# FFN products of a float32 kernel: one 512-column matmul for both input parts over the high weights, and the down product by output tiles behind all gate and up products

## The chip, the cores and the metric

One core of one Trainium2 chip. The time is device microseconds of one launch on that core, the median of several runs; profiles are of one execution.

## The reference

Two transformer blocks in float32 on 256 tokens of width 1024, with a hidden width of 2816 in the feed-forward networks (FFN). What the change touches are five FFNs:

```python
def conv_ffn(h, w_up, dw_w, dw_b, w_down):          # block 1, once
    u = causal_dwconv(h @ w_up, dw_w) + dw_b        # 3 taps over tokens
    gt, v = jnp.split(u, 2, axis=-1)
    return (jax.nn.silu(gt) * v) @ w_down

def swiglu(x, w_gate, w_up, w_down):                # block 2, four times
    return (jax.nn.silu(x @ w_gate) * (x @ w_up)) @ w_down
...
x = layer_norm(ALPHA * x + 0.5 * swiglu(x, ...), g, b)
```

Around them stand a conformer convolution module (first block), an RWKV-7 mixer with memory attention and a stick-breaking attention with memory attention (second block), and a norm over features after each part.

## The kernel before

Activations lie feature-major: 128 features on partitions, 8 tiles (`KD`) of 256 tokens (`T`). TensorE works on fp32r operands, and each float32 operand is split in a high part, rounded to fp32r, and a low part, the rest. A product of two such operands is three matmuls, high x high, high x low and low x high; low x low is left out. That is `mm3` (L359 to L363): weights stationary (128x128), the activation moving (256 columns).

Weights come as units of 128x1024 float32 in the order of use, two to a DMA of 1 MB on SP's queue (`Stream`, L191). ScalarE casts a unit to its high part `whi` (L229), VectorE subtracts to get the low part `wlo` (L238). `take()` hands out the next unit and issues the splits of the units up to four ahead (`LEAD`); there are 7 buffers for `whi`, 6 for `wlo`. A unit feeds 24 matmuls in every product.

An FFN (`ffn`, L631) goes over 22 hidden tiles j. For each: two units, gate and up, through `gemm_out` into the two halves of one PSUM bank `gu` (48 matmuls), then one unit of the down product of tile j-2 through `gemm_acc` into all 8 output tiles, which are held in 4 banks `acc` (24 matmuls), then the gate of tile j. `ffn_gate` (L672) makes silu(gate) x up on ScalarE and VectorE in three steps and splits it into `hh` and `hl`; its steps are issued between the products (`advance`), so that the engines' queues don't block. The first two tiles run together in `gemm_outs` (L378), one input tile after the other, as the norm before delivers them. The last four hidden tiles are added in `gemm_tail` (L420), one output bank after the other, so that the first output tiles go through their residual add and their squares while the others are still in product.

`Norm` (L1109) sums outputs and squares over tiles: tiles 0 to 3 on GpSimd, 4 and 6 on VectorE, `merge` adds the two, tiles 5 and 7 go as they are; `finish` (L1150) sums over partitions with matmuls of one column on TensorE, issues 12 products that nothing uses (L348), computes the deviation, and broadcasts it over partitions with transposes into `bc` (L1188). `ln_out` (L522) and, in the conv FFN, `rms_scale` apply it tile by tile (L530, L555), and the next product starts on the first tile.

In PSUM there are 8 banks: 2 `gu`, 4 `acc`, 2 for statistics. The order of all work is written out by hand; each engine runs its queue in order.

Of the kernel before, what the change touches and what calls it, by code (L numbers as in the profile page):

```python
# [76 lines left out]
def constants():  # L77
    """Masks and selectors, which depend on the shapes only."""
# [23 lines left out]
def lay_out(inp, parts=ALL):  # L102
    """Host layout: every array sent holds input elements only, reordered."""
# [25 lines left out]
    def ffn(g, u, w):  # L129
        g, u, dn = out_major(g), out_major(u), k_major(w)  # L130
        o = []
        for j in range(NF):
            o += [g[j], u[j]]
            if 0 <= j - 2 < NF - 4:
                o.append(dn[j - 2])
        return np.concatenate([np.stack(o), tail(w)])
# [54 lines left out]
class Stream:  # L191
    """Weight units in the order of use: loaded ahead two by two, then split into two fp32r parts."""
# [18 lines left out]
    def split(self, upto):  # L211
        """split units below upto; ScalarE is one unit ahead of VectorE."""
# [33 lines left out]
    def take(self, ahead=True):  # L246
        """(hi, lo) of the next unit."""
# [6 lines left out]
class Builder:  # L254
# [26 lines left out]
    def open_x(self):  # L281
        """the operand tiles of the dense products; closed where a mixer needs their space."""
        self.xpool = ExitStack()
        xp = self.xpool.enter_context(self.pool("x", side="right"))
        self.xh, self.xl = (xp.tile([P, KD, T], F32R, name=n) for n in ("xh", "xl"))

# [17 lines left out]
    def enter_dense(self, tmp=True):  # L304
        """PSUM banks for the accumulators and the statistics."""
# [28 lines left out]
    def fill(self, n, warm):  # L334
        """n steps of the memory's products, while TensorE would wait for a norm."""
# [5 lines left out]
    def keep_warm(self, n):  # L341
        """products that nothing uses: the clock of TensorE halves when it idles."""
# [8 lines left out]
    def pump(self, us):  # L351
        """issue background work of VectorE for about this long."""
# [6 lines left out]
    def mm3(self, out, wh, wl, xh, xl, start, stop):  # L359
        mm = self.nc.tensor.matmul  # L360
        mm(out, lhsT=wh, rhs=xh, start=start, stop=False, skip_group_check=True)  # L361
        mm(out, lhsT=wh, rhs=xl, start=False, stop=False, skip_group_check=True)  # L362
        mm(out, lhsT=wl, rhs=xh, start=False, stop=stop, skip_group_check=True)  # L363

    def gemm_out(self, ps, xh, xl):
        """one output tile of 128 features from the next unit."""
        for _ in self.gemm_out_parts(ps, xh, xl):
            pass

    def gemm_out_parts(self, ps, xh, xl):  # L370
        wh, wl = self.stream.take()
        for k in range(KD):
            c = slice(k * P, k * P + P)
            self.mm3(ps, wh[:, c], wl[:, c], xh[:, k, :], xl[:, k, :], k == 0, k == KD - 1)
# [3 lines left out]
    def gemm_outs(self, banks, xh, xl):  # L378
        """two output tiles in each bank, from the input tiles as they come."""
        mm = self.nc.tensor.matmul  # L380
        ws = [self.stream.take() for _ in range(2 * len(banks))]
        for k in range(KD):
            c = slice(k * P, k * P + P)
            for q in range(3):
                for i, (wh, wl) in enumerate(ws):
                    mm(banks[i // 2][:, i % 2, :], lhsT=(wh, wl, wh)[q][:, c],  # L386
                       rhs=(xh, xh, xl)[q][:, k, :], start=k == 0 and q == 0 and i % 2 == 0,
                       stop=k == KD - 1 and q == 2, skip_group_check=True)

    def gemm_tok(self, ps, xh, xl, u):  # L390
# [1620 lines left out]
```

## Time and profile before

| | us |
|---|---|
| runs | 1525.16, 1525.85, 1528.46; median 1525.85 |
| profiled execution, from the first to the last instruction | 1528.2 |
| TensorE busy in it | 1472.2 |
| VectorE, ScalarE, GpSimd busy in it | 987.6, 788.0, 86.5 |

Of the profiled execution only the span from the first to the last instruction is given, so it is set against the median of the runs by its ratio. Engines work side by side, so busy times don't add up. TensorE has two rows: PE for matmuls, PEld for weight loads, which run under matmuls. Matmuls are pipelined, and their durations overlap: the time that one costs is the distance from its start to the next one's.

### The profile page before, as it was taken

The page shows a single profiled execution, that of the slowest core. Times are in us where ns is not written, and L with a number is a line of the kernel's source. Part 1 is how long each engine was busy: PE and PEld are TensorE (multiplying, and loading weights), DVE is VectorE, ACT ScalarE, POOL GpSimd, SP SyncE. Part 2 cuts the span into 40 slices and gives each one's busy share as a digit, 9 for nine tenths or more (in the row PEclk, how much of TensorE's full clock was granted, in tenths as well). Part 3 has the DMA queues.
Part 4 walks back from the last instruction along what each step waited for, and adds up shares of the span by engine and source line. Part 5 has one row for each costly group of instructions (what it writes and reads, how often), then busy time and mean ns, then how long its engine had stood idle before and what let it go on. Part 6 is the DMA issues. An engine that isn't in the chain of part 4 may idle for free.

```text
span 1528.2 us, 30494 instructions
## 1 busy us (share of the span) xinstructions
PE 1472.2 (96%) x13109; PEld 1416.0 (93%) x13109; DVE 987.6 (65%) x1493; ACT 788.0 (52%) x1251; POOL 86.5 (6%) x74
## 2 busy tenths in 40 slices
PE   8888899999999999989999999999999999999997
PEld 7867899999999998878889999999999988999997
DVE  8897787776655458985567555575454855664554
ACT  7697466665544446530245444454444566454443
POOL 1110100000000010130010000100000111100001
PEclk9999899999999999999989999999999999999998
DMA  9785366563655543320034555445554433265540
GB/s 384 267 269 200 112 228 228 178 208 112 218 174 188 193 138 132 111 84 3 2 111 169 190 190 176 160 165 184 180 190 166 147 111 104 90 232 184 192 166 28
DMA packets 39161, 250.66 MB, mean 164 GB/s; under 512 B 4337, under 2 KB 4849, under 8 KB 12274
## 3 DMA queue, kind: packets, MB, share of 16 engines
q1 hardware_dynamic: 38594, 247.60, 46.6%
q8 instruction: 102, 1.67, 0.4%
q10 hardware_dynamic: 432, 1.11, 0.2%
q14 instruction: 33, 0.27, 0.1%
HBM read 247.65 MB, written 1.05 MB: 163 GB/s over the span
## 4 chain that ended last, share of the span: by engine, by line
PE 81%; DVE 12%; ACT 4%; issue 2%; POOL 1%; DMA 0%; DVEq 0%; ACTq 0%; POOLq 0%
PE gu L361 14%; PE gu L363 13%; PE gu L362 13%; PE acc L361 7%; PE acc L362 7%; PE acc L363 7%; PE acc L386 3%; DVE wlo L238 2%; PE r L1653 2%; PE st L1161 1%; DVE mraw L570 1%; PE gu L1236 1%; PE gu L348 1%; DVE ys L530 1%; ACT whi L229 1%
## 5 line engine op out<-in xcount | busy, mean ns | idle before, releaser
L238 DVE TENSOR_TENSOR wlo<-wraw,whi 128x1024 fp32r<-128x1024 f32 x416 | 512.4, 1239 | 294.2 <-PE gu L363 152.1
L229 ACT CAST whi<-wraw 128x1024 fp32r<-128x1024 f32 x416 | 430.0, 1047 | 186.7 <-PE gu L362 116.8
L361 PE MATMUL gu<-xh,whi 128*128 128x256 f32 x1824 | 516.1, 283 | 0.0
L363 PE MATMUL gu<-xh,wlo 128*128 128x256 f32 x1824 | 511.5, 280 | 0.0
L362 PE MATMUL gu<-xl,whi 128*128 128x256 f32 x1824 | 508.0, 278 | 0.0
L361 PEld LDWEIGHTS gu<-xh,whi 128*128 128x128 f32 x1824 | 343.2, 188 | 8.8 <-issue 8.4
L362 PEld LDWEIGHTS gu<-xl,whi 128*128 128x128 f32 x1824 | 343.3, 188 | 0.7 <-issue 0.7
L363 PEld LDWEIGHTS gu<-xh,wlo 128*128 128x128 f32 x1824 | 342.4, 188 | 0.0
L362 PE MATMUL acc<-hl,whi 128*128 128x256 f32 x880 | 248.8, 283 | 0.1
L361 PE MATMUL acc<-hh,whi 128*128 128x256 f32 x880 | 248.9, 283 | 0.0
L363 PE MATMUL acc<-hh,wlo 128*128 128x256 f32 x880 | 248.5, 282 | 0.0
L362 PEld LDWEIGHTS acc<-hl,whi 128*128 128x128 f32 x880 | 168.0, 191 | 0.4 <-DVE hl L700 0.3
L363 PEld LDWEIGHTS acc<-hh,wlo 128*128 128x128 f32 x880 | 168.1, 191 | 0.0
L361 PEld LDWEIGHTS acc<-hh,whi 128*128 128x128 f32 x880 | 167.7, 191 | 0.1
L695 ACT ACTIVATE sg<-gu 128x256 f32<-128x256 f32 x80 | 30.7, 384 | 159.6 <-PE gu L363 159.6
L1138 POOL TENSOR_TENSOR nsum<-ys 128x512 f32<-128x512 f32 (+1 forms) x9 | 12.2, 1359 | 1178.9 <-ACT ys L1121 1178.9
L698 ACT CAST hh<-h 128x256 fp32r<-128x256 f32 x110 | 44.7, 407 | 62.5 <-DVE h L697 62.5
L570 DVE TENSOR_TENSOR mraw<-mraw,cact 128x1024 f32<-128x1024 f32 x48 | 60.0, 1252 | 0.4 <-DMA mraw<-in_mod 0.3
L687 DVE SCALAR_TENSOR_TENSOR u<-gu,vecs,u 128x255 f32<-128x255 f32 (+1 forms) x80 | 33.1, 476 | 35.0 <-ACT u L682 35.0
L574 ACT ACTIVATE mraw<-mraw 128x1024 f32<-128x1024 f32 x48 | 50.4, 1054 | 4.2 <-DVE mraw L570 4.2
L700 DVE TENSOR_TENSOR hl<-h,hh 128x256 fp32r<-128x256 f32 x110 | 46.1, 419 | 7.1 <-ACT hh L698 7.1
L697 DVE TENSOR_TENSOR h<-gu,sg 128x256 f32<-128x256 f32 x80 | 33.4, 418 | 20.7 <-ACT sg L695 20.7
(349 smaller groups left out, 2028.5 us busy)
## 6 DMA issues: line engine op xcount, KB each, us to landing
wraw<-in_w SPq DMA_DIRECT2D x208, 1024.0 KB, 4.9
mraw<-in_mod SPq DMA_DIRECT2D x48, 512.0 KB, 5.6
xr<-in_x SPq DMA_DIRECT2D x2, 512.0 KB, 4.1
m<-in_mem SPq DMA_DIRECT2D x1, 1024.0 KB, 8.2
out<-xr SPq DMA_DIRECT2D x3, 256.0 KB, 2.5
cst<-in_consts SPq DMA_DIRECT2D x1, 546.0 KB
lora<-in_lora ACTq DMA_DIRECT2D x1, 384.0 KB, 3.1
lora_g<-in_lora ACTq DMA_DIRECT2D x1, 384.0 KB, 3.8
```

What stands on the lines that cost most here:

```text
L229: b.nc.scalar.copy(out=hi, in_=raw)
L238: b.nc.vector.tensor_tensor(out=lo, in0=raw, in1=hi.bitcast(F32), op=ALU.subtract)
L361: mm(out, lhsT=wh, rhs=xh, start=start, stop=False, skip_group_check=True)
L362: mm(out, lhsT=wh, rhs=xl, start=False, stop=False, skip_group_check=True)
L363: mm(out, lhsT=wl, rhs=xh, start=False, stop=stop, skip_group_check=True)
L386: mm(banks[i // 2][:, i % 2, :], lhsT=(wh, wl, wh)[q][:, c], rhs=(xh, xh, xl)[q][:, k, :], start=k == 0 and q == 0 and i % 2 == 0, stop=k ...
L570: self.nc.vector.tensor_tensor(out=raw, in0=raw, in1=self.cact, op=ALU.mult)
L574: self.nc.scalar.activation(out=raw, in_=raw, func=AF.Copy, accum_out=self.mod[:, j:j + 1])
L687: nc.vector.scalar_tensor_tensor(out=u[i][:, sh:], in0=gu[:, i, :T - sh], scalar=self.vec("f_dw_w", tap * 2 * NF + j + i * NF), in1=u[i][: ...
L697: nc.vector.tensor_tensor(out=h, in0=up, in1=sg, op=ALU.mult)
L698: nc.scalar.copy(out=hh, in_=h)
L700: nc.vector.tensor_tensor(out=hl, in0=h, in1=hh.bitcast(F32), op=ALU.subtract)
```

## The change

The two parts of an activation now lie side by side in one tile, `xx[:, k]` of shape [128, 2, 256], and so do those of a hidden tile, `hx`. Two new helpers: `mm_lo` multiplies the low weights with the high part into the first half of a bank; `mm_wide` does that and then one matmul of 512 columns, high weights with both parts, into the whole bank. So a bank now holds one output tile, in two halves that must be added.

- Gate and up of the four SwiGLU FFNs run through `gemm_wide` (first two tiles `gemm_wides`), each with its own bank; three pairs of banks take turns (`acc` 0 and 1, `acc` 2 and 3, the two `gu`). `wide_gate` copies the second half of each bank with ScalarE and adds the first half with VectorE.
- In the conv FFN gate and up keep three matmuls and one bank.
- In all five FFNs the down product no longer runs between the gates: it follows when all 22 hidden tiles are issued, output tile by output tile, 22 `mm_wide` each, through the four `acc` banks in turn. The steps of the last gate are issued behind products 4 and 8 of the first output tile. The down weights are laid out for this order; a unit still has 8 blocks of 128x128.
- Each output tile adds its two halves as it ends (`on_tile`: in the SwiGLU FFNs two VectorE operations, in the conv FFN a ScalarE copy and a VectorE add), its square follows, and GpSimd sums tiles 0 to 5; tiles 6 and 7 go to the statistics as they are. `gemm_tail` remains for the mixers' output projections.
- The modulation work that was pumped in during the conv FFN's gates (`pump`) is issued between its output tiles.

```diff
+        self.xx = xp.tile([P, KD, 2, T], F32R, name="xx")
+        self.xh, self.xl = self.xx[:, :, 0, :], self.xx[:, :, 1, :]
...
+    def mm_lo(self, out, wl, x, start):
+        self.nc.tensor.matmul(out, lhsT=wl, rhs=x[:, 0, :], start=start, stop=False,
+                              skip_group_check=True)
...
+    def mm_wide(self, bank, wh, wl, x, start, stop):
+        self.mm_lo(bank[:, 0, :], wl, x, start)
+        self.nc.tensor.matmul(bank, lhsT=wh, rhs=x, start=False, stop=stop, skip_group_check=True)
...
+    def gemm_wide(self, bank, x):
+        wh, wl = self.stream.take()
+        for k in range(KD):
+            c = slice(k * P, k * P + P)
+            self.mm_wide(bank, wh[:, c], wl[:, c], x[:, k], k == 0, k == KD - 1)
...
+    def gemm_wides(self, banks, x):
+        ws = [self.stream.take() for _ in banks]
+        for k in range(KD):
+            c = slice(k * P, k * P + P)
+            for bank, (_, wl) in zip(banks, ws):
+                self.mm_lo(bank[:, 0, :], wl[:, c], x[:, k], k == 0)
+            for bank, (wh, _) in zip(banks, ws):
+                self.nc.tensor.matmul(bank, lhsT=wh[:, c], rhs=x[:, k], start=False, stop=k == KD - 1,
+                                      skip_group_check=True)
...
             for j in range(2, NF):
-                gu = self.gu_tile()
+                bk = banks(j)
                 for o in range(2):
-                    self.gemm_out(gu[:, o, :], self.xh, self.xl)
+                    if conv:
+                        self.gemm_out(bk[0][:, o, :], self.xx)
+                    else:
+                        self.gemm_wide(bk[o], self.xx)
                     advance()
-                if acc is None:
-                    acc = [self.acc_tile(i) for i in range(4)]
-                if j - 2 < NF - self.NT:
-                    self.gemm_acc(acc, *hs.pop(0), j == 2)
-                gate(j, gu)
-                if j % 2:
-                    self.pump(1.0)
-            advance()
-            advance()
+                gate(j, bk)
             self.preload(AF.Sqrt)
-            self.gemm_tail(acc, [h[0] for h in hs], [h[1] for h in hs], st, on_tiles)
+            i = 0
+            for o in range(KD):
+                acc = self.acc_tile(o % 4)
+                for j in range(NF):
+                    if i % 8 == 0:
+                        wh, wl = self.stream.take()
+                    c = slice(i % 8 * P, i % 8 * P + P)
+                    self.mm_wide(acc, wh[:, c], wl[:, c], hs[j], j == 0, j == NF - 1)
+                    i += 1
+                    if o == 0 and j in (4, 8):
+                        advance()
+                on_tile(o, acc)
+                st.square(o, o + 1)
+                st.sum(o, o + 1, "pool")
+                if o < KD - 1:
+                    self.pump(3.0)
...
+    def wide_gate(self, banks, j, hh, hl):
+        nc = self.nc
+        lows = self.fp.tile([P, 2, T], F32, name="lows", tag="lows", bufs=2)
+        gs = self.fp.tile([P, 2, T], F32, name="gs", tag="gs", bufs=2)
+        g, u = gs[:, 0, :], gs[:, 1, :]
+        nc.scalar.copy(out=lows[:, 0, :], in_=banks[0][:, 1, :])
+        nc.vector.tensor_tensor(out=g, in0=banks[0][:, 0, :], in1=lows[:, 0, :], op=ALU.add)
+        nc.scalar.copy(out=lows[:, 1, :], in_=banks[1][:, 1, :])
+        nc.scalar.activation(out=g, in_=g, func=AF.Silu)
+        yield
+        nc.vector.tensor_tensor(out=u, in0=banks[1][:, 0, :], in1=lows[:, 1, :], op=ALU.add)
+        nc.vector.tensor_tensor(out=u, in0=u, in1=g, op=ALU.mult)
+        nc.scalar.copy(out=hh, in_=u)
+        yield
+        nc.vector.tensor_tensor(out=hl, in0=u, in1=hh.bitcast(F32), op=ALU.subtract)
...
+        def on_tile(k, ps):
+            y = self.ys[:, k, 0, :]
+            self.nc.vector.scalar_tensor_tensor(out=y, in0=self.xr[:, k, :], scalar=2 * ALPHA,
+                                                in1=ps[:, 1, :], op0=ALU.mult, op1=ALU.add)
+            self.nc.vector.tensor_tensor(out=y, in0=ps[:, 0, :], in1=y, op=ALU.add)
```

## Rows read from the trace of the kernel before

**Rows 1.** The page: busy time of the engines, and the chain that ended last.
```profile
PE 1472.2 (96%) x13109; PEld 1416.0 (93%) x13109; DVE 987.6 (65%) x1493; ACT 788.0 (52%) x1251; POOL 86.5 (6%) x74
PE 81%; DVE 12%; ACT 4%; issue 2%; POOL 1%; DMA 0%; DVEq 0%; ACTq 0%; POOLq 0%
```

**Rows 2.** Busy time by stretch: the conv FFN, then the first SwiGLU FFN.
```profile
core 0: us, PE busy (x) PEld busy (x) DVE busy (x) ACT busy (x) POOL busy (x), PEclk, DMA share, GB/s
181.00:367.00 186.00, 185.11 (x1573) 184.47 (x1571) 144.22 (x223) 116.88 (x182) 2.86 (x3) 1.00 0.56 190
374.00:563.00 189.00, 187.99 (x1584) 187.55 (x1583) 104.83 (x130) 89.37 (x121) 4.37 (x3) 1.00 0.52 179
```

**Rows 3.** Groups by line and shape: count | busy us, mean ns of one.
```profile
L362 PE MATMUL gu<-xl,whi 128*128 128x256 f32 x1824 | 508.0, 278 | 0.0
...
L361 PE MATMUL acc<-hh,whi 128*128 128x256 f32 x880 | 248.9, 283 | 0.0
...
L238 DVE TENSOR_TENSOR wlo<-wraw,whi 128x1024 fp32r<-128x1024 f32 x416 | 512.4, 1239 | 294.2 <-PE gu L363 152.1 <-PE acc L363 49.1 <-issue 45.8
...
L229 ACT CAST whi<-wraw 128x1024 fp32r<-128x1024 f32 x416 | 430.0, 1047 | 186.7 <-PE gu L362 116.8 <-PE acc L362 58.0 <-DMA wraw<-in_w 5.5
...
L697 DVE TENSOR_TENSOR h<-gu,sg 128x256 f32<-128x256 f32 x80 | 33.4, 418 | 20.7 <-ACT sg L695 20.7
L695 ACT ACTIVATE sg<-gu 128x256 f32<-128x256 f32 x80 | 30.7, 384 | 159.6 <-PE gu L363 159.6
```

**Rows 4.** Timeline of TensorE in the first SwiGLU FFN: start us, us.
```profile
429.82 0.28 PE L363 MATMUL gu<-xh,wlo 128*128 128x256 f32 x1
...
434.88 0.28 PE L361 MATMUL acc<-hh,whi 128*128 128x256 f32 x1
...
437.76 0.28 PE L361 MATMUL gu<-xh,whi 128*128 128x256 f32 x1
```

**Rows 5.** Timeline of TensorE in the stick-breaking mixer: float32 products of two passes.
```profile
1224.82 0.59 PE L1966 MATMUL z<-e,sbc 128*128 128x256 f32 x2
1225.25 0.38 PE L1967 MATMUL z<-e,negones 128*128 128x128 f32 x2
1225.47 0.39 PE L1969 MATMUL z<-e,sbc 128*128 128x128 f32 x2
```

**Rows 6.** Groups by line and shape: a float32 pass of 128 columns.
```profile
L1967 PE MATMUL z<-e,negones 128*128 128x128 f32 x24 | 4.6, 274 | 0.0
```

**Rows 7.** The chain that ended last, after the second SwiGLU FFN's down product.
```profile
990.61 1.69 DVE nsum L1138
...
993.14 3.17 PE st L1161 x16
996.31 2.77 PE gu L348 x12
999.08 0.87 PE bc L1188 x4
```

**Rows 8.** Timeline of TensorE there: the last matmul, then one-column matmuls.
```profile
991.31 0.28 PE L363 MATMUL acc<-hh,wlo 128*128 128x256 f32 x1
991.43 0.95 PE L1161 MATMUL st<-inv,ys 128*128 128x1 f32 x8
```

**Rows 9.** Timeline and chain: end of the conv FFN, then of the last FFN.
```profile
366.59 0.28 PE L363 MATMUL acc<-hh,wlo 128*128 128x256 f32 x1
...
371.65 0.44 PE bc L1188 x2
...
1513.40 0.28 PE L363 MATMUL acc<-hh,wlo 128*128 128x256 f32 x1
...
1513.68 2.85 PE st L1161 x24
...
1517.68 1.13 PE bc L1188 x4
```

More of the change, by code (lines that the diff above doesn't have):

```diff
@@ L624, in memory_steps, with ffn, gate @@
         for o in range(2):
-            yield from self.gemm_out_parts(self.mem_ps[0][:, o, :], self.mh, self.ml)
+            yield from self.gemm_out_parts(self.mem_ps[0][:, o, :], self.mx)
             yield
         for u in range(2):
-            yield from self.gemm_tok(self.mem_ps[1], self.mh, self.ml, u)
-    def ffn(self, conv, st, on_tiles):
+            yield from self.gemm_tok(self.mem_ps[1], self.mx, u)
+    def ffn(self, conv, st, on_tile):
         self.mark("ffn")
         with self.pool("ffn") as self.fp:
-            first = [self.acc_tile(2), self.acc_tile(3)]
-            self.gemm_outs(first, self.xh, self.xl)
-            hs, gates = [], []
-            acc = None
-            def gate(j, gu):
-                hs.append([self.fp.tile([P, T], F32R, name=n, tag=n, bufs=self.NT + 1)
-                           for n in ("hh", "hl")])
-                gates.append(self.ffn_gate(gu, j, conv, *hs[-1]))
+            hs = [self.fp.tile([P, 2, T], F32R, name=f"hx{j}") for j in range(NF)]
+            gates = []
+            def gate(j, banks):
+                make = self.conv_gate if conv else self.wide_gate
+                gates.append(make(banks, j, hs[j][:, 0, :], hs[j][:, 1, :]))
                 next(gates[-1])
@@ L649, in advance, with banks @@
                         gates.remove(g)
-            for j, gu in enumerate(first):
-                gate(j, gu)
+            def banks(j):
+                if conv:
+                    return [self.acc_tile(2 + j) if j < 2 else self.gu_tile()]
+                return [self.gu_tile() for _ in range(2)] if j % 3 == 2 else [
+                    self.acc_tile(2 * (j % 3) + o) for o in range(2)]
+            first = [banks(0), banks(1)]
+            (self.gemm_outs if conv else self.gemm_wides)(first[0] + first[1], self.xx)
+            for j, bk in enumerate(first):
+                gate(j, bk)
                 advance()
@@ new lines, in ffn @@
+                gate(j, bk)
+            self.mark("down")
+            self.preload(AF.Sqrt)
+            i = 0
[14 more added lines that the diff above has]
+                    self.pump(3.0)
@@ new lines, in conv_gate @@
+    def conv_gate(self, banks, j, hh, hl):
+        nc = self.nc
+        gu, = banks
+        sg, h = u = [self.fp.tile([P, T], F32, name=f"u{i}", tag=f"u{i}", bufs=2) for i in range(2)]
+        for i in range(2):
+            f = j + i * NF
+            nc.scalar.activation(out=u[i], in_=gu[:, i, :], func=AF.Identity,
+                                 scale=self.vec("f_dw_w", 2 * 2 * NF + f), bias=self.vec("f_dw_b", f))
+        for tap, sh in ((1, 1), (0, 2)):
+            for i in range(2):
+                nc.vector.scalar_tensor_tensor(
+                    out=u[i][:, sh:], in0=gu[:, i, :T - sh],
+                    scalar=self.vec("f_dw_w", tap * 2 * NF + j + i * NF), in1=u[i][:, sh:],
+                    op0=ALU.mult, op1=ALU.add)
+        yield
+        nc.scalar.activation(out=sg, in_=u[0], func=AF.Silu)
+        nc.vector.tensor_tensor(out=h, in0=u[1], in1=sg, op=ALU.mult)
```

127 lines of the change are left out of this document (50 added, 77 removed).

## The prediction

> **What bounds the kernel now.** Read the page first. TensorE is busy for 1472 of 1528 us and holds 81% of the chain that ended last [rows 1]. Second, the table by stretch, for the feed-forward (FFN) stages: in the conv FFN TensorE is busy 185.1 of 186 us, in the first SwiGLU FFN 188.0 of 189 us, at a granted clock of 1.00, which is 2.4 GHz; VectorE there is busy 144 and 105 us, ScalarE 117 and 89 us [rows 2]. So in an FFN nothing but the products counts, and anything else is worth something only where TensorE waits. Five FFNs of about 188 us are 62% of the span.
>
> Third, the groups of instructions, for counts and kinds: 1824 calls of `mm3` from gate, up and input projections, 880 from the down products, each with three matmuls of 256 columns and three weight loads [rows 3]. Fourth, the timeline of TensorE inside an FFN, for the spacing of matmuls, since the durations of 0.28 us overlap: 43 matmuls of gate and up from 429.82 to 434.88 us are 117.7 ns apart, 24 of the down product from 434.88 to 437.76 us are 120.0 ns apart [rows 4]. 256 columns at 2.4 GHz are 106.7 ns. So each matmul costs 11.0 (gate, up) or 13.3 ns (down) above its columns. That excess is what the change works on; the columns stay.
>
> **Part 1: one wide product in place of two.** Before, a step is 3 matmuls x 256 columns; after, it is one of 256 (low weights) and one of 512 (high weights, both input parts). Columns: 768 in both. It is done for gate and up of the four SwiGLU FFNs, 4 x 44 units x 8 = 1408 steps, and for all five down products, 5 x 22 x 8 = 880 steps. The conv FFN's gate and up keep three matmuls, as do the projections.
>
> The trace has no 512-column matmul of this type, so its spacing is bounded. Lower bound: a float32 product of the mixer shows two passes for each call, and its passes take 110 ns for 128 columns (L1967, 0.22 us for two) but 215 ns for 256 (L1966, 0.43 us from 1224.82 to 1225.25) [rows 5], half the column rate. So such a pass over 256 columns lasts as long as 512 columns would here: 512 cycles at 2.4 GHz (213.3 ns) and 2 ns. Upper bound: two of today's, 235.4 (gate, up) or 240 ns (down) [rows 4], no gain. Middle: the excess is paid once per matmul whatever its width: 213.3 + 11.0 = 224.3, or 213.3 + 13.3 = 226.6 ns.
>
> Which of the three is nearest depends on what the excess is. One candidate is the weight load: a matmul of a single column has nothing to stream, and eight of them still take 0.95 us, 0.11 us apart [rows 8], so a weight load alone paces at about 0.11 us; under a 512-column stream it would be hidden, which gives the lower bound. Against it speaks the duration of one matmul: a half-rate pass of 128 columns, also 256 cycles and also with a weight load behind each, lasts 274 ns [rows 6] and starts 110 ns after the one before (0.22 us for two [rows 5]), while the 256-column products last 278 to 283 ns [rows 3]. The stream itself is longer by 4 to 9 ns, not just its wait for weights. I take the middle: fixed for each matmul.
>
> Then gate and up save 11.0 ns x 1408 = 15.5 us and the down products 13.3 ns x 880 = 11.7 us: 27.2 us. At the lower bound a wide matmul replaces 235.4 by 215 and 240 by 215: 20.4 x 1408 + 25 x 880 = 50.7 us. At the upper bound 0.
>
> The Trainium skill (TensorE: Matmul & The Clock Gate, section "Back-to-back issue gap") gives an isolated gap of N/2.4 + 2.5 ns, 262 cycles for 256 columns and 518 for 512. For 256 columns this trace disagrees, 117.7 ns [rows 4] against its 109; for 512 cycles it agrees with the 215 ns of [rows 5]. By that rule the sum would be the 50 us of the lower bound; it is the first rival below.
>
> **Part 2: gates.** A wide bank holds two halves that must be added: `wide_gate` adds two ScalarE copies and two VectorE adds for each j to the two and two there. At 384 and 418 ns [rows 3] that is 22 x 0.8 = 18 us per FFN on each engine. All gate and up work now stands in 22 x 16 steps, 120 us at 342 ns. In it ScalarE does 44 casts (1047 ns), 46 us, plus 22 x 4 x 0.4 = 35 us: 81 of 120 us. VectorE does 44 subtractions (1239 ns), 55 us, plus 37 us: 92 of 120 us. TensorE's own 120 us hides both; three sets of banks in turn give each gate two further j, 11 us, before its bank is wanted. Without that cover the added 18 us would stand in each FFN. In the conv FFN, gate and up alone are 22 x 48 x 117.7 = 124 us; VectorE had 144 us in the whole stage, and 22 of its 66 subtractions (27 us) and the modulation work move to the down part, so less than 117 of 124 us stay. Priced at nothing. The weights come in units of 24 matmuls' worth in either order, and the SP queue loads the same bytes at the same rate: nothing.
>
> **Part 3: the seam.** The first output tile needs all 22 hidden tiles. The last gate's remaining steps are issued behind products 4 and 8 of that tile; its chain (copy, add, Silu, table load, one cast, add, product, cast, subtraction, at 0.4 to 1.3 us) is some 5.5 us, and TensorE comes to product 21 after 21 x 0.345 = 7.2 us. Priced at nothing; if it is 2 us late, 10 us over five FFNs.
>
> **Part 4: the end of each FFN.** Today tiles 4 to 7 end within a few us of each other and VectorE must sum them: after the last matmul of the second SwiGLU FFN (FFN 2) starts (991.31 [rows 8]) the chain shows a VectorE sum of 1.69 us and more, 16 statistics matmuls, 12 fillers of which the last end at 999.08, then the broadcast until 999.95 [rows 7]: 8.64 us. After the change tile 7 ends 7 us behind tile 6, GpSimd has the six sums long before, and what is left is two VectorE steps instead of one, a square (0.42 each), four matmuls (0.7 with their drain), the 1.15 us seen between statistics and broadcast in the last FFN (1516.53 to 1517.68 [rows 9]) and the broadcast, 0.5 to 0.9, with 0.39 for the wide matmul itself and 0.2 of hand-overs: 4.5 us, or 6 if the clock falls and the fillers take 2.8 us as in [rows 7]. FFN 2 saves 2.6 to 4.1 us; the last FFN took 5.41 and the conv FFN 5.50 [rows 9], which leaves 0 to 1 each (in the conv FFN a table load now stands behind the Silu of the last gate); the first and third SwiGLU FFN I put between these, at 1 to 2. Sum 8 us, bounds 4 to 11.
>
> **Sum.** 1528.2 - 27.2 - 8 = 1493.0 us for the profiled execution. Its span is 1528.2 us and the page shows nothing around it; the runs' median is 1525.85, 0.15% below. 1493.0 x 0.9985 = 1491 us.
>
> **Rivals.**
> 1. The excess is the hand-over behind a weight load and vanishes under a long stream (for it [rows 5, 8], against it [rows 3, 6]): 50.7 + 8, so 1528.2 - 58.7 = 1469.5, 1467 us.
> 2. The change does not do what it says: the excess belongs to the columns, a stream at full rate being fed a little too slowly. For it: half-rate streams show almost none [rows 5, 6]. Against it: gate and down differ (117.7 and 120.0) with the same columns. Only part 4 is left: 1518 us.
> 3. Slower: a feed that is too slow may run dry in a long stream. If the wide matmul's second half were read at the half rate of L1966, it would take 107 + 215 = 322 ns, 85 ns above two of today's, and 2288 of them cost 195 us: 1710 us. It decides from 240 ns per wide matmul on, where 3.5 ns x 2288 eats the 8 us of part 4. No row shows such a feed; every 256-column stream lasts about the same.
> 4. The seam and the gates cost what I put at nothing: 10 to 25 us, 1501 to 1516 us.
>
> **How the numbers follow.** Forecast 1491 with chance 0.48 (with 1480 to 1500 as its own range); rival 1 0.28; rival 2 0.11; rival 4 0.08; rival 3 0.05. The range reaches down past rival 1 (bound of part 4: 1464) and up to 1510, which leaves out rivals 2 and 3 and the end of 4. A difference of 0.2% is about what measurement of this kernel can tell from none. Faster 0.91, same 0.04 (rival 2 with nothing from part 4), slower 0.05.
>
> **What would show it.** A wide matmul followed by the next at 224 to 227 ns, and steps of 342 to 347 ns; FFNs of about 181 us against 188; TensorE still busy throughout each FFN, VectorE and ScalarE below it; no wait of TensorE for the last hidden tile; after the last product of an FFN, 4.5 to 6 us to the broadcast. A spacing of 215 would mean rival 1, of 235 rival 2, beyond 240 rival 3; gaps of TensorE on gate tiles rival 4. Wrong above all would be the assumption that the excess is paid per matmul.

## The result, and the profile after

The changed kernel takes 1508.45 us (median of 4 runs, 1506.64 to 1513.66) against 1525.85: 0.9889 of the time before, 95% interval [0.9866, 0.9911]. A second series of it, in the first experiment, gave 1509.08 and 0.9887 [0.9871, 0.9902]. So it is faster by 17 us, 1.1%. The forecast was 1491 us; the direction and the range (1464 to 1510) held, but the gain is just under half of the 35 us worked out.

The page first (the profiled execution spans 1511.9 us):

```profile
PE 1455.1 (96%) x10821; PEld 1300.6 (86%) x10821; DVE 1076.0 (71%) x1701; ACT 832.4 (55%) x1447; POOL 103.3 (7%) x84
...
PE 82%; DVE 12%; ACT 4%; issue 2%; DMA 1%; POOL 0%; DVEq 0%; ACTq 0%; POOLq 0%
```

TensorE is as much the bound as it was in [rows 1]: 2288 matmuls fewer, and only 17 us less of its time. The groups by line and shape (count | busy us, mean ns of one) show what the new matmul is:

```profile
L370 PE MATMUL acc<-hx,whi 128*128 128x512 f32 x880 | 310.8, 398 | 0.0
...
L370 PE MATMUL acc<-xx,whi 128*128 128x512 f32 x832 | 289.6, 390 | 0.0
L358 PE MATMUL gu<-xx,wlo 128*128 128x256 f32 x992 | 278.8, 281 | 0.0
L358 PE MATMUL acc<-hx,wlo 128*128 128x256 f32 x880 | 247.4, 281 | 0.0
```

Durations overlap, so the cost is read from the spacing, as in [rows 4]. The timeline of TensorE in the first SwiGLU FFN, three steps of a gate or up product and three of the down product:

```profile
439.73 0.28 PE L358 MATMUL gu<-xx,wlo 128*128 128x256 f32 x1
439.85 0.39 PE L370 MATMUL gu<-xx,whi 128*128 128x512 f32 x1
...
440.77 0.28 PE L358 MATMUL gu<-xx,wlo 128*128 128x256 f32 x1
...
530.07 0.28 PE L358 MATMUL acc<-hx,wlo 128*128 128x256 f32 x1
530.19 0.40 PE L370 MATMUL acc<-hx,whi 128*128 128x512 f32 x1
...
531.13 0.28 PE L358 MATMUL acc<-hx,wlo 128*128 128x256 f32 x1
```

Three steps take 1.04 us in gate and up and 1.06 in the down product. From the unrounded starts a step (one low and one wide matmul, called a pair below) is 346.7 ns (118.3 low + 228.3 wide) and 353.3 ns (116.7 + 236.7 in the mean). Three matmuls of before took 353.1 and 360.0 ns. So a step saves 6.4 to 6.7 ns, where 11.0 and 13.3 were forecast.

The table by stretch: the conv FFN, ten microseconds inside it, and the first SwiGLU FFN, beside [rows 2]:

```profile
core 0: us, PE busy (x) PEld busy (x) DVE busy (x) ACT busy (x) POOL busy (x), PEclk, DMA share, GB/s
178.00:371.00 193.00, 189.89 (x1428) 181.69 (x1426) 148.92 (x231) 123.29 (x195) 5.43 (x5) 0.99 0.52 189
200.00:210.00 10.00, 7.71 (x53) 7.53 (x53) 8.37 (x15) 7.37 (x13) 0.00 (x0) 0.83 0.36 117
376.50:563.20 186.70, 185.74 (x1060) 162.63 (x1060) 129.30 (x185) 98.85 (x167) 8.22 (x5) 1.00 0.52 186
```

The SwiGLU FFN is full of products, with VectorE and ScalarE well below. The conv FFN has lost TensorE time near 204 us, and some clock with it (0.83 over those ten microseconds). From first to last product (in the conv FFN from the products of the memory on, right behind the broadcast), and from the last matmul's start to the end of the broadcast, in us, each in the one profiled execution:

| FFN | products before | after | end before | end after |
|---|---|---|---|---|
| conv | 189.72 | 192.24 | 5.48 | 4.77 |
| SwiGLU 1 | 189.32 | 186.19 | 7.04 | 4.94 |
| SwiGLU 2 | 188.70 | 185.67 | 8.62 | 4.94 |
| SwiGLU 3 | 188.70 | 185.66 | 6.48 | 5.66 |
| SwiGLU 4 | 188.69 | 185.66 | 5.40 | 4.79 |

SwiGLU products give 12.2 us, the ends 7.9, and the conv FFN takes 2.5 back: 17.6. (The conv FFN also starts 1.1 us later in this execution; the profiled span is 16.3 us shorter.) The end of the second SwiGLU FFN in the timeline, to be held against [rows 7, 8]:

```profile
986.16 0.40 PE L370 MATMUL acc<-hx,whi 128*128 128x512 f32 x1
...
986.40 0.95 PE L1219 MATMUL st<-inv,ys 128*128 128x1 f32 x8
986.60 0.42 DVE L1100 SCALAR_TENSOR_TENSOR ys<-xr,acc 128x256 f32<-128x256 f32 x1 [4.25 <-PE acc L370]
...
987.51 0.42 ACT L1179 ACTIVATE ys<-ys 128x256 f32<-128x256 f32 x1 [5.47 <-DVE ys L1102]
...
988.10 1.03 PE L1219 MATMUL st<-inv,ys 128*128 128x1 f32 x8
...
989.00 1.66 PE L346 MATMUL gu<-whi 128*128 128x256 f32 x12
...
990.50 0.60 PE L1246 MATMUL bc<-head,rn 128*128 128x128 f32 x4
```

VectorE's sum of 1.69 us is gone: it had been idle for 4.25 us when the last tile came. Two adds and a square (L1100, its neighbour L1102, and L1179) run while TensorE does the statistics that were ready before; the last tile's follow at 988.10. 990.50 + 0.60 - 986.16 = 4.94 us against 8.62.

The loss in the conv FFN, in the timeline of all engines:

```profile
201.53 2.00 ACT L226 CAST whi<-wraw 128x1024 fp32r<-128x1024 f32 x2
...
201.99 2.35 DVE L235 TENSOR_TENSOR wlo<-wraw,whi 128x1024 fp32r<-128x1024 f32 x2
...
203.43 1.01 ACT L738 ACTIVATE u<-gu,vecs 128x256 f32<-128x256 f32 x2
...
203.70 0.28 PE L358 MATMUL gu<-xx,wlo 128*128 128x256 f32 x1
...
204.47 1.65 DVE L742 SCALAR_TENSOR_TENSOR u<-gu,vecs,u 128x255 f32<-128x255 f32 x4
...
206.27 0.55 PE L363 MATMUL gu<-xx,whi 128*128 128x256 f32 x1 [2.29 <-ACT u L747]
```

The third gate's steps (L738, L742) stand behind casts and subtractions of weights, 2.00 us on ScalarE and 2.35 on VectorE. They read one of only two banks that gate and up have from there on; TensorE wants that bank again at 203.82; its last reader, L742, ends at 206.12 (the row names L747 as releaser, ScalarE's next step, which ends about then but doesn't read the bank). From the matmul at 203.70 to the next are 2.57 us, 2.45 of them waiting. The granted clock falls to half at the end of that wait (0.50 from 206.2 to 209.6 us, which is 1.2 GHz), and the 14 matmuls behind the one at 206.27 stand 213 ns apart instead of 118.

### The profile page after: what moved, and what is told of

Its sections match the earlier page's. It is cut to its first block, busy times and chain, and to the rows that moved or that the text cites. A ratio compares the mean times of both kernels' runs of the same rounds, so it can differ in the third digit from the quotient of the medians.

```text
span 1511.9 us, 26295 instructions
## 1 busy us (share of the span) xinstructions
PE 1455.1 (96%) x10821; PEld 1300.6 (86%) x10821; DVE 1076.0 (71%) x1701; ACT 832.4 (55%) x1447; POOL 103.3 (7%) x84
## 4 chain that ended last, share of the span: by engine, by line
PE 82%; DVE 12%; ACT 4%; issue 2%; DMA 1%; POOL 0%; DVEq 0%; ACTq 0%; POOLq 0%
PE acc L370 26%; PE acc L358 15%; PE gu L358 7%; PE gu L370 7%; PE gu L363 4%; PE gu L364 3%; DVE wlo L235 2%; PE r L1711 2%; PE acc L412 2%; DVE mraw L595 2%; PE st L1219 1%; PE gu L1294 1%; DVE ys L555 1%; PE gu L346 1%; ACT whi L226 1%
## 5 line engine op out<-in xcount | busy, mean ns | idle before, releaser
L370 PE MATMUL acc<-hx,whi 128*128 128x512 f32 x880 | 310.8, 398 | 0.0
L358 PE MATMUL acc<-xx,wlo 128*128 128x256 f32 x1088 | 292.8, 284 | 2.9 <-ACT xx L561 1.6
L370 PE MATMUL acc<-xx,whi 128*128 128x512 f32 x832 | 289.6, 390 | 0.0
L358 PE MATMUL gu<-xx,wlo 128*128 128x256 f32 x992 | 278.8, 281 | 0.0
L358 PE MATMUL acc<-hx,wlo 128*128 128x256 f32 x880 | 247.4, 281 | 0.0
L358 PEld LDWEIGHTS acc<-xx,wlo 128*128 128x128 f32 x1088 | 201.2, 190 | 8.5 <-ACT xx L561 4.4
L358 PEld LDWEIGHTS gu<-xx,wlo 128*128 128x128 f32 x992 | 187.6, 189 | 0.2
L358 PEld LDWEIGHTS acc<-hx,wlo 128*128 128x128 f32 x880 | 166.1, 189 | 0.0
L363 PE MATMUL gu<-xx,whi 128*128 128x256 f32 x544 | 158.3, 291 | 2.3 <-ACT u L747 2.3
L364 PE MATMUL gu<-xx,whi 128*128 128x256 f32 x544 | 152.6, 281 | 0.0
L1179 ACT ACTIVATE ys<-ys 128x256 f32<-128x256 f32 (+1 forms) x66 | 28.6, 437 | 157.5 <-DVE ys L1102 140.6
L363 PEld LDWEIGHTS gu<-xx,whi 128*128 128x128 f32 x544 | 103.0, 189 | 11.2 <-issue 8.4
L364 PEld LDWEIGHTS gu<-xx,whi 128*128 128x128 f32 x544 | 103.1, 189 | 0.7 <-issue 0.7
L370 PEld LDWEIGHTS gu<-xx,whi 128*128 128x128 f32 x448 | 84.1, 188 | 17.7
L1100 DVE SCALAR_TENSOR_TENSOR ys<-xr,acc 128x256 f32<-128x256 f32 x32 | 13.5, 421 | 95.0 <-PE acc L370 95.0
```

What stands on the lines that cost most here:

```text
L358: self.nc.tensor.matmul(out, lhsT=wl, rhs=x[:, 0, :], start=start, stop=False, skip_group_check=True)
L363: mm(out, lhsT=wh, rhs=x[:, 0, :], start=start, stop=False, skip_group_check=True)
L364: mm(out, lhsT=wh, rhs=x[:, 1, :], start=False, stop=False, skip_group_check=True)
L370: self.nc.tensor.matmul(bank, lhsT=wh, rhs=x, start=False, stop=stop, skip_group_check=True)
L1179: b.nc.scalar.activation(out=b.ys[:, k0:k1, 1, :], in_=y, func=AF.Square)
```

## The experiments

The theories at the start: **A**, the excess over the columns belongs to the columns (rival 2 of the prediction), so a wide matmul has twice of it; **B**, it is paid once for each matmul, as predicted, and what more is seen comes from the other engines' traffic in these stages; **C**, it comes from the place of the operands. Beside them, what the conv FFN's wait and the ends of the FFNs are worth.

**1. The changed kernel, unaltered.**

> The changed kernel once more, unaltered, timed beside the next two. Both theories: 1506 to 1510 us, ratio to the kernel before 0.987 to 0.991.

1509.08 us (1508.1 to 1510.74), ratio 0.9887 [0.9871, 0.9902]. The pause in the conv FFN (193.05 us) is there again, 2.56 us from the start at 202.9 to the next, the step spacings too; the five ends are 4.12, 4.94, 5.79, 4.94 and 4.79 us, 24.6 in all. The pause and the spacings are the kernel's, not one execution's; the ends differ by 0.9 us in single FFNs.

**2. Trains of matmuls on idle tiles,** 96 of each kind, placed behind the last output.

```diff
+            for i in range(N):
+                mm(o[0][:, :256], lhsT=w[:, c(i)], rhs=x[:, i % 8, 0, :], start=i == 0, stop=i == N - 1, skip_group_check=True)
...
+            for i in range(N):
+                mm(o[0], lhsT=w[:, c(i)], rhs=x[:, i % 8], start=i == 0, stop=i == N - 1, skip_group_check=True)
```

> The changed kernel with ten trains of matmuls on idle tiles behind its last output, nothing else running: fp32r of 256, 384 and 512 columns, 512 columns from a second tile, 256 and 512 in turn from either tile, 512 with the same weights throughout, bf16 of 256 and 512. Theory A (the excess over the columns grows with their number, because a stream of 4-byte columns is fed a little slower than 2.4 GHz): 256 at 117 to 120 ns, 384 at about 172, 512 at about 228, whatever the weights, and bf16 512 at about 216. Theory B (the excess is paid once per matmul, and the 228 to 237 ns seen in the changed kernel come from other engines' traffic): 384 at 171, 512 at 224 or below when alone. Theory C (the place of the moving tile counts): the two tiles differ by several ns at the same width.

The timeline of TensorE puts each train in one row, so that the start of the next less its own start, over 96, is the spacing (the window read ends within the train of 384 columns, so that its row counts 11 here):

```profile
1517.82 11.47 PE L1144 MATMUL bo<-xx,bw 128*128 128x256 f32 x96
1529.13 2.11 PE L1146 MATMUL bo<-xx,bw 128*128 128x384 f32 x11
...
1546.09 22.56 PE L1148 MATMUL bo<-xx,bw 128*128 128x512 f32 x96
1568.49 21.95 PE L1150 MATMUL bo<-bh,bw 128*128 128x512 f32 x96
1590.27 0.28 PE L1152 MATMUL bo<-xx,bw 128*128 128x256 f32 x1
...
1679.88 10.65 PE L1160 MATMUL bo<-bhb,bwb 128*128 128x256 bf16 x96
1690.37 20.88 PE L1162 MATMUL bo<-bhb,bwb 128*128 128x512 bf16 x96
```

256 columns: 117.8 ns; 384: 176.7; 512: 233.3 and, from a second tile, 226.9. The same block of weights throughout takes 233.4 for 512 columns, no less than eight blocks in turn. The excess is 11.1, 16.7, and 20.0 or 13.6 ns: it grows with the columns, with every other engine idle. bf16 with the same sizes takes 109.3 and 215.8 (the last from the starts within the train), an excess of 2.5 ns at both widths. For bf16 that is the Trainium skill's isolated gap of N/2.4 + 2.5 (TensorE: Matmul & The Clock Gate, section "Back-to-back issue gap"), 109.2 and 215.8; for the fp32r products of this kernel the runs disagree with it, by 8.6 ns at 256 columns and 11 to 18 at 512. Pairs of a low and a wide matmul took 118.3 + 228.3 from one tile and 116.7 + 236.7 from the other, the kernel's two spacings; which looked like C, and is taken up in 7 to 9. A holds in the main (its 172 for 384 columns was too low); B is out, as 384 and 512 columns exceed its 171 and 224 with nothing else running.

**3. The new order with narrow products:** each wide matmul as two of 256 columns.

```diff
-        self.nc.tensor.matmul(bank, lhsT=wh, rhs=x, start=False, stop=stop, skip_group_check=True)
+        for h in range(2):
+            self.nc.tensor.matmul(bank[:, h, :], lhsT=wh, rhs=x[:, h, :], start=False, stop=stop,
+                                  skip_group_check=True)
```

> Every wide matmul of the changed kernel split again into two of 256 columns with the same weights; order, banks, gates and norm stay as changed. It sets apart what the width gives from what the new order gives. Theory A and B alike by the spacings of the two profiles: steps of 353 ns instead of 346.7 in gate and up, 360 instead of 353 in down, so 1408 x 6.3 + 880 x 6.6 = 14.7 us slower than the changed kernel, about 1523 us, 2 to 4 us under the kernel before. Rival (the new order itself slows the products, by reading the hidden tiles from another place): 1530 us or more.

1523.9 us (1517.74 to 1528.79, 12 runs), ratio 0.9981 [0.9967, 0.9994], against 0.9887 for the changed kernel timed beside it: the width is worth 0.94%, 14.4 us, give or take 3 (each ratio is good to 0.0015). By the spacings of the kernel before it is 1408 x 6.4 ns = 9.0 us for gate and up, 704 x 6.7 = 4.7 for the SwiGLU down products and, by this run's profile, 176 x 4.9 = 0.9 for the conv FFN's (356.0 to 351.1 ns a step): 14.6. This profile shows one thing more: the same three narrow matmuls of gate and up take 353.3 ns in the first and third SwiGLU FFN and 350.0 in the second and fourth, so that its own spacings give 12.6. The new order by itself gains 2.5 us in the medians. In the profiles it gains 7.0: the ends come to 25.2 us (before 33.0), the SwiGLU products are 1.0 us shorter in all, and the conv FFN, which has the pause too (2.66 us at 203.6), is 1.9 longer. But the profile before is of a long execution: 1528.2 us, where the 17 executions of that kernel timed here span 1522.5 to 1529.1. How much of the 7.0 us an average execution has is not shown.

**4. Four banks for gate and up of the conv FFN.** Hidden tiles with j % 4 over 1 go to the two accumulator banks that are idle until the down product.

```diff
-                    return [self.acc_tile(2 + j) if j < 2 else self.gu_tile()]
+                    return [self.acc_tile(2 + j) if j < 2 else self.acc_tile(j % 4 - 2) if j % 4 > 1
+                            else self.gu_tile()]
```

> The conv FFN's gate and up take four banks in turn (two of them free accumulators) instead of two; nothing else is altered. Theory (the stall of 2.6 us of TensorE near 204 us is a wait for a bank that the third gate still reads, and the half clock of 3.4 us after it costs 1.6 us more): 4 us faster than the changed kernel, 1504 us, no gap over 0.5 us and no half clock between 180 and 370 us. Rival (VectorE and ScalarE are simply too slow there, the wait only moves on): less than 1 us.

1510.6 us (1508.8 to 1512.45), 0.9896 [0.9879, 0.9912]: nothing gained beside the unaltered kernel. The wait at 203 is gone and the conv FFN is 190.55 us instead of 193.05, but the five ends come to 27.0 us instead of 24.6 (5 and 6 take that up), and a new wait stands at the seam. The timeline, all engines:

```profile
307.55 1.28 ACT L324 ACT_TABLE_LOAD   x1
...
310.01 1.28 ACT L748 ACT_TABLE_LOAD   x1
...
312.00 0.39 PE L370 MATMUL acc<-hx,whi 128*128 128x512 f32 x1
...
313.23 0.42 DVE L752 TENSOR_TENSOR hx<-u,hx 128x256 fp32r<-128x256 f32 x1
...
313.70 0.50 PE L370 MATMUL acc<-hx,whi 128*128 128x512 f32 x1 [0.65 <-DVE hx L752]
```

ScalarE brings in the table for Sqrt (L324), and 2.5 us later needs the one for Silu again (L748) for the last gate, whose hidden tile comes at 312.6 (high part) and 313.65 (low part). TensorE needed it at 312.2, and the down products take 1.4 us longer.

**5. The Sqrt table behind the last gate's Silu,** on top of 4.

```diff
-            self.preload(AF.Sqrt)
             i = 0
...
+                    if o == 0 and j == 8:
+                        self.preload(AF.Sqrt)
```

> The four banks of the run before, and the Sqrt table is asked for behind the last gate's Silu instead of ahead of it. In the run with four banks TensorE stood 2.0 us at the last hidden tile of the conv FFN (a table load of 1.28 us for the Silu stood in that gate's chain). Theory: that gap goes, the conv FFN takes 188.5 us against 193.0 in the changed kernel; by time 4 us faster than the changed kernel, 1505 us, unless the clock falls in more of the norms (up to 1.6 us each). Rival (VectorE is behind by then and the gap stays): 1508 us or more.

The conv FFN is down to 189.12 us, with no wait but that of its start, 3.9 less than unaltered. The kernel takes 1509.91 us (1505.51 to 1510.86), 0.988 [0.986, 0.9899]: unchanged. In its profile the five ends take 5.19, 4.94, 7.00, 6.49 and 5.14 us, 28.8 against 24.6. The stretch at the end of the second SwiGLU FFN in the table by stretch (columns as in the one above), then its timeline:

```profile
981.00:989.00 8.00, 8.00 (x49) 7.95 (x47) 2.31 (x8) 2.37 (x5) 0.00 (x0) 0.65 0.03 14
```

```profile
983.00 1.44 PE L1221 MATMUL st<-inv,ys 128*128 128x1 f32 x8
984.30 2.91 PE L346 MATMUL gu<-whi 128*128 128x256 f32 x12
...
985.59 0.16 DVE L1245 SCALAR_TENSOR_TENSOR rn<-st,rn 128x2 f32<-128x2 f32 x1
...
987.00 1.05 PE L1248 MATMUL bc<-head,rn 128*128 128x128 f32 x4
```

The granted clock fell to half at 983.45, while TensorE did 24 matmuls of one column. The 12 fillers behind them take 2.91 us instead of 1.66, so that the broadcast starts at 987.00, though its input was ready at 985.75: the fillers, there to hold the clock, come after its fall and are themselves waited for. The fall does not come each time: the first SwiGLU FFN of the same execution ends with the same 24 matmuls at a clock of 1.00, in 4.94 us. (The half clock lasts 6.8 us at this end and 3.4 at that of the third.)

**6. Fewer statistics and earlier fillers,** on top of 5, in the FFN norms. Tile 6 goes into GpSimd's sum, so that 8 one-column matmuls fall away (4 in the conv FFN), and 8 fillers stand ahead of the last tile's statistics.

```diff
-            if eng is None or self.n > KD - 2:
+            if eng is None or self.n > KD - self.late:
...
         for i, s in enumerate(srcs):
+            if self.warm and i == len(srcs) - 1:
+                b.keep_warm(self.warm)
```

> The version before this one (four banks, table load moved) took its conv FFN from 193.05 to 189.12 us, and yet its time stayed at 1509.9: its five ends of FFNs took 28.8 us instead of 24.6, with the granted clock at half for 6.8 us in two of them. Here the second last output tile goes into GpSimd's running sum, so that 8 one-column matmuls fall away at each end, and 8 products that nothing uses (8 x 0.118 = 0.94 us) stand in their place, ahead of the last tile's statistics. Theory (the gain of the conv FFN was lost again to the clock in the ends): the clock stays up, the ends come to 4.1 to 4.9 us each, 20.5 to 24.5 in all, and the kernel takes 1503 to 1506. Rival (the clock falls for what comes before the end, or the ends move for some other reason): ends of 26 us and more, falls of the clock as before, 1508 to 1511. A second rival: the statistics of the last tile are put off by the products in front of them, and the ends grow by up to 0.9 us each: 1510 to 1514.

1505.33 us (1504.52 to 1508.07), 0.9872 [0.9851, 0.9893]. The five ends are 4.12, 5.00, 5.00, 5.00 and 4.36 us, 23.5. The same table and timeline of the same place:

```profile
979.00:987.00 8.00, 7.04 (x57) 6.65 (x55) 4.27 (x14) 3.48 (x7) 0.00 (x0) 1.00 0.19 78
```

```profile
980.08 1.20 PE L346 MATMUL gu<-whi 128*128 128x256 f32 x8
...
981.11 0.95 PE L1224 MATMUL st<-inv,ys 128*128 128x1 f32 x8
981.92 1.67 PE L346 MATMUL gu<-whi 128*128 128x256 f32 x12
```

The clock stays at 1.00 and the fillers take 1.67 us again. By the times alone the step from 5 to 6 is not settled, as the two intervals overlap; and the clock in the ends differs between executions (the unaltered kernel's end of the third SwiGLU FFN took 5.66 and 4.94 us in its two profiles). The other traces settle it. In the eight profiles of the new order without these fillers (the one after, experiments 1 to 5, 7 and 8) the granted clock fell to half within 19 of the 32 ends of the first four FFNs; in the three with them (6, 9 and 10) in none of 12. Where it does not fall, a SwiGLU end takes the same either way, 4.94 and 5.00 us. So the first theory holds: the ends had eaten the conv FFN's gain, through the clock. Whether the fewer statistics or the earlier fillers hold it was not tried apart.

**7. Where the operands stand.** Trains of 48 with the moving operand at ten offsets, weights at five, and weight loads of 64 columns instead of 128.

```diff
+                    mm(o[:cols, :n], lhsT=w[:, ws], rhs=big[:, off:off + n], start=i == 0, stop=i == N - 1,
+                       skip_group_check=True)
```

> The changed kernel with trains of 48 matmuls on idle tiles behind its last output: 512 columns from one tile at ten offsets from 0 to 8 KB (weights in turn), the same columns with one fixed block of weights at five places, 256 columns at two places, and 256 and 512 columns with 64 columns of weights instead of 128. Theory A1 (the slow feed is the moving stream's own): offsets change 512 columns by no more than the 227 to 234 ns seen, and half the weight load changes nothing. Theory A2 (the weight load's reads hold up the stream): with 64 weight columns 256 fall from 118 to about 113 and 512 from 228 to about 221; offsets that put weights and stream together are slowest.

The timeline's last trains: wte with 512 columns, na and nb with 256, then the halved weight loads nc (256 columns) and hc (512):

```profile
1673.06 11.04 PE L1147 MATMUL wte<-big,bw 128*128 128x512 f32 x48
1683.94 5.92 PE L1147 MATMUL na<-big,bw 128*128 128x256 f32 x48
1689.69 5.92 PE L1147 MATMUL nb<-big,bw 128*128 128x256 f32 x48
1695.45 5.61 PE L1147 MATMUL nc<-big,bw 128*64 128x256 f32 x48
1700.90 11.20 PE L1147 MATMUL hc<-big,bw 128*64 128x512 f32 x48
```

512 columns: 226.7 ns (10.88 us / 48) from the sixth train on, at the five offsets from 128 to 2048 floats and with one block of weights throughout, at each of five places. The first five trains (offsets 0, 8, 16, 32 and 64) had 227.3, 233.4, 229.1, 232.2 and 227.7 ns; those at 8, 16 and 32 kept this to their end, and these offsets were not run again, so that for them place is not excluded here. Halving the weight load takes nothing off 512 columns (229.8, from the starts within the train) but brings 256 columns from 119.8 to 113.5. So the stream itself costs 226.7 ns for 512, 544 cycles at 2.4 GHz, and 113.5 for 256, half of that; and at 256 the weight load adds 4 to 7 ns. That answers the prediction's question between weight load and stream: both have a part.

**8. The pair, by place.**

```diff
+                    mm(o[:, :256], lhsT=w[:, lo + c:lo + c + P], rhs=x[:, a:a + 256], start=i == 0,
+                       stop=False, skip_group_check=True)
+                    mm(o, lhsT=w[:, c:c + P], rhs=x[:, a:a + 512], start=False, stop=i == N - 1,
+                       skip_group_check=True)
```

> Trains of a low (256 columns) and a wide (512 columns) matmul in turn, 48 pairs each, after the last output, on idle tiles; a train's moving operand stands at offset 0, 16, 256, 512, 1024, 2048 or 4096 floats of one tile (pa to pg), then again at 0, 512, 256, 2048, 0 (ph to pl); ra to rd walk on by 512 floats with each pair, rc with its low weights in other columns, rd, re and rf with the operand tile of the gate and up products. In the kernel a pair takes 346.7 ns in the gate and up products and 353.3 in the down products. Theory P (the place of the moving operand sets it): one offset gives one pitch, 346.7 or 353.3, the same each time that it comes back. Theory Q (the pattern in which weight loads and matmuls fall into step at the start of a train sets it, not the place): the same offset gives different pitches when it comes back, or all offsets give the same one. Theory R (walking on through the tile costs): ra to rd differ from pa to pg.

The first train (offset 0) ran at 353.5 ns for a pair, the second at 348.9, and all sixteen others settled at 346.7, among them offset 0 again, twice, and the walks through the tile. So place is not it (P and R fall), as far as offsets came back; that of the second train, 16 floats, did not. The pattern that a train falls into is what is left (Q).

**9. A disturbance ahead of each output tile of the down products,** on top of 6: one matmul that nothing uses, of 64, 128, 192, 256, 32, 96 or 160 columns ahead of tiles 1 to 7.

```diff
                 acc = self.acc_tile(o % 4)
+                self.nudge(NUDGE[o], hs[0])
```

> On the version with four banks, the moved table and the fillers, a matmul that nothing uses stands ahead of output tiles 1 to 7 of each down product, with 64, 128, 192, 256, 32, 96 and 160 columns. In the version without them a pair of a low and a wide matmul takes 353.3 ns through the whole of a SwiGLU FFN's down product (in a pattern that comes back every three pairs) and 351.2 in the conv FFN's, where the gate and up products and the settled trains of the run before take 346.7. Theory Q (the step in which weight loads and matmuls fall in at the start sets the pitch, and it stays until something disturbs it): after some of the seven disturbances the pitch goes to 346.7 and stays there until the next one; if all tiles went there the down products would be 880 x 6.6 = 5.8 us shorter, less about 0.5 us in each FFN for the added matmuls. Rival (something in the down products holds them at 353, such as the separate tiles of their operand or eight weight blocks to a unit): the pitch returns to 353.3 or 351.2 within each tile, and the kernel gets 2 to 3 us longer.

One execution, 1508.45 us. The mean spacing of a pair in each tile, from the trace (the last 18 of its 21 spacings), in ns:

| tile | 0 | 1 | 2 | 3 | 4 | 5 | 6 | 7 |
|---|---|---|---|---|---|---|---|---|
| columns of the added matmul | 0 | 64 | 128 | 192 | 256 | 32 | 96 | 160 |
| first SwiGLU FFN | 353.3 | 346.7 | 353.3 | 353.3 | 353.3 | 346.7 | 353.3 | 346.7 |
| conv FFN | - | 351.1 | 350.7 | 350.6 | 351.1 | 350.7 | 350.6 | 350.6 |

All four SwiGLU FFNs agree to 0.1 ns. Three of the disturbances (64, 32 and 160 columns) bring the spacing of the gate and up products, and it stays for the tile. Behind the other four it is 353.3: 192 and 256 columns leave it there, 128 and 96 bring it back from 346.7. In the conv FFN none changes more than 0.5 ns, so there Q is not shown.

**10. One disturbance for each SwiGLU FFN,** that of 64 columns ahead of tile 1.

```diff
-NUDGE = (0, 64, 128, 192, 256, 32, 96, 160)
+NUDGE = (0, 64, 0, 0, 0, 0, 0, 0)
...
-                self.nudge(NUDGE[o], hs[0])
+                self.nudge(0 if conv else NUDGE[o], hs[0])
```

> Of the seven disturbances of the run before, only the one of 64 columns ahead of output tile 1, and only in the four SwiGLU FFNs. There it took the pair from 353.3 to 346.7 ns for the whole of its tile. Theory Q (the step stays until something disturbs it): tiles 1 to 7 run at 346.7, 154 pairs x 6.6 = 1.02 us less in each of the four FFNs, less 0.03 for the matmul itself, so 4.0 us in all: an FFN of 184.7 instead of 185.67 us, and 1500.5 to 1502.5 for the kernel, where the version without it took 1505.33. Rival (the step drifts back within a tile or two): 353.3 again in the later tiles, 1504.5 to 1505.5.

1501.74 us, 0.9839 [0.9826, 0.9852]: five of six executions lie between 1501.38 and 1502.84; the sixth took 7908.11, which nothing here explains, and the comparison leaves it out. The timeline at the start of tile 1 and near the end of the same tile in the first SwiGLU FFN:

```profile
504.35 0.19 PE L721 MATMUL gu<-hx 128*128 128x64 f32 x1
...
511.06 0.28 PE L359 MATMUL acc<-hx,wlo 128*128 128x256 f32 x1
...
511.75 0.28 PE L359 MATMUL acc<-hx,wlo 128*128 128x256 f32 x1
```

Two pairs take 0.69 us from 511.06 on. Tile 0 runs at 353.3 ns a pair, tiles 1 to 7 at 346.7 to the last. The SwiGLU FFNs take 185.30, 184.76, 184.76 and 184.77 us, 0.9 less each, and the kernel 3.6 less than in 6 (4.0 expected). This version beats both kernels: 24 us below the one before, 7 below the changed one (0.9839 against 0.9887).

## Why the prediction was half wrong

**Part 1 failed, in its choice of the middle: the term of 27.2 us was nearly twice too large.** "The excess is paid once per matmul whatever its width" gave 224.3 and 226.6 ns for the wide matmul; it takes 228.3 and 236.7. Some 60% of the excess, 6.7 of 11.0 ns for 256 columns, belongs to the stream and doubles with it (226.7 ns for 512 columns, also with one block of weights throughout); the rest comes with the weight load and is what the wide matmul saves: 14.4 us instead of 27.2. In the SwiGLU down products the slower of two spacings stands on top of that (236.7 instead of 228.3). The prediction had the sign of it in hand: from the durations it read that "the stream itself is longer by 4 to 9 ns", and then took the excess as fixed, though a stream that is itself longer would be expected to be so in proportion to its columns. Rival 2 ("the excess belongs to the columns") had the larger half of the truth, and its argument, that half-rate streams show almost no excess, was in [rows 5]: those 215 ns were float32 passes, whose columns are fed at half the rate, and said nothing about the feed at full rate. The argument held against it, that gate and down differ with the same columns, was no argument: the same instructions fall into different spacings, 346.7 and 353.3 ns for a pair (experiments 8 to 10) and 350.0 and 353.3 for three narrow matmuls (experiment 3). That the 120.0 of the narrow down products is such a spacing too was not tried. Rival 1 (215 ns) is wrong for fp32r: no train of 512 columns went below 226.7; it holds for bf16. Rival 3 had its threshold at 240 ns per wide matmul, and the down product came to 236.7, 3 ns short of it; what saved it there was as much the low matmul beside it, 116.7 ns instead of 120.0.

**Part 2 was right for the SwiGLU FFNs and wrong for the conv FFN.** VectorE and ScalarE have room, 129 and 99 of 187 us. By spacing the SwiGLU FFNs should gain 13.7 us and gain 12.2. The 1.5 us missing are not gates: the first two hidden tiles of each take longer, 13.3 us instead of 13.1 in the first FFN and 12.8 instead of 12.4 in the others (1.4 in all), and TensorE waits there for input tiles of the norm, most for a low part that the first wide matmul needs (0.61 us in the second FFN, where before no wait was over 0.32):

```profile
805.25 1.20 PE L412 MATMUL acc<-xx,whi 128*128 128x512 f32 x4 [0.61 <-DVE xx L573]
```

The prediction had no term for that start. In the conv FFN the sum over the stage ("less than 117 of 124 us") was no proof: for the first gates, which come together behind the norm's end, the two banks are too few, and the wait and the half clock after it cost some 4 us (experiments 4 and 5). This is the second step that failed: a wait priced at nothing. Rival 4 had named such a cost, at 10 to 25.

**Part 3, the seam, was right** in the changed kernel, which has no wait there. In the conv FFN it held only because the earlier wait had thrown the products back: with that gone the last hidden tile came 1.4 us late (experiment 4).

**Part 4 was right in kind, and its size partly luck:** 8 us forecast, 7.9 measured between the two profiled executions. In the second SwiGLU FFN 1.69 of the 3.68 us are VectorE's sum, as it said; about 1.1 more are the 12 fillers, 2.77 us under the fallen clock of [rows 7] and 1.66 at full clock after. With the clock the five ends took 24.6 to 29.4 us together in five executions of the changed kernel (the profile after, experiments 1, 2, 7 and 8), and single ends up to 6.9 us, above the 6 allowed for.

Summed up, us:

| | forecast | measured |
|---|---|---|
| wide products | -27.2 | -14.6 (spacings; -14.4 by experiment 3) |
| gates and banks, in the SwiGLU FFNs the start | 0 | +3.4 in the conv FFN, +1.5 in the others |
| seam | 0 | 0 |
| ends of the FFNs | -8 | -7.9 |
| sum | -35.2 | -17.6 |

Left open: what about the pattern of weight loads and matmuls makes 346.7, 351.1 or 353.3 ns of the same pair; why the conv FFN's down product doesn't move; and why the clock falls at the same end in one execution and not in another.

## What to carry to other kernels

Before counting on a wider matmul, split the excess of the narrow one: time a train of it, one with half the weight load, and one of the width in question, in the same type, for only the part that comes with the weight load is saved. Busy shares over a stage don't show a burst: where banks are few, follow the first two or three users of each through the engines' queues. What depends on the granted clock is read in several executions, not in one. And a wait that is removed on a bound engine is a gain only if the next one, here a table load and then the clock in the norms, isn't waiting behind it.

## What the runs showed of the hardware that was not expected

- An fp32r matmul of 128 weight columns streams 512 columns in 226.7 ns at best, 544 cycles at a granted clock of 1.00, and bf16 in 215.8; the 6% over 512 cycles are paid per column (113.5 ns for 256 with a weight load of 64 columns).
- A pair of low and wide matmuls has at least two stable spacings, 346.7 ns and a pattern of three pairs (349, 350 and 361 ns from wide to wide matmul) with a mean of 353.3, at the same operands; it held over 170 pairs, and one added matmul of 64 columns switched it for the 154 pairs that followed, worth 0.9 us in each FFN.
- With 24 one-column matmuls (12 in the conv FFN) behind the products and fillers only after them, the granted clock fell to half within 19 of 32 ends of FFNs (0.65 over 8 us in one of them); with 16 (8) and 8 products of 256 columns between, it stayed at 1.00 in 12 of 12.
